# One merge-gate product of the convolution branch, computed among the indexer's scores

## The chip, the core and the metric

The kernel runs on one core of a Trainium2 chip. The metric is the device time of one execution in microseconds. A core has a matrix engine (PE, with its weight loads as PEld), a vector engine (DVE), an activation engine (ACT), a general engine (POOL) and an engine that issues transfers (SP). Each works through its own instruction list strictly in order, and an instruction whose input isn't there holds up all behind it on its engine.

## The reference, cut to what matters

One decoder block on 1024 tokens and 16 meta tokens (L = 1040), width 1024. Between two feed-forward halves stands a hybrid mixer:

```python
q, k, v, qi, ki, wi, u, gate_b, gate_c, g_att, g_conv = jnp.split(h @ w_in, offs, axis=-1)
# indexer: I[t,s] = sum_h wi[t,h] relu(qi[t,h] . ki[s]); keep the 256 best causal keys; GQA attention on them
s = jax.nn.relu(jnp.einsum('bthd,bsd->bths', qi, ki))
score = jnp.einsum('bths,bth->bts', s, wi)
y_att = att @ w_att_out
y_conv = (gate_b * short_conv(gate_c * u, conv_w)) @ w_conv_out
merged = jax.nn.sigmoid(g_att) * y_att + jax.nn.sigmoid(g_conv) * y_conv
return merged @ w_o
```

The product in question is an eighth of `g_conv = h @ w_in[:, O_GB:]`: 128 of its 1024 channels, for all 1024 real tokens.

## The kernel before

Activations lie as channels by tokens, every float32 operand split into a high and a low part, so that a product is three matmuls a step (`hi*xh`, `hi*xl`, `lo*xh`). A weight slab of 1024x128 is loaded by SP into a tile `raw` (L147), rounded by ACT into `hi` (L142), and its rest put into `lo` by DVE or POOL (L143). Times 1024 tokens that is 2 halves x 8 steps x 3 = 48 matmuls of 512 columns (L169 to L171, into a bank `ps`). The slabs of one pool (`slots`) go through two buffers each of `raw`, `hi` and `lo`; a third load waits until the first is used up.

The stages that the change touches, in their order:

1. Indexer queries (`queries`, O_QI): products, rotary on DVE, casts `rh` on ACT and rests `rl` on DVE, then stores of both to DRAM (`qis`, L747, issued by SP). Each store has 32 partitions x 4 heads x 512 tokens. Then the values (`values`): products, copies `v_t` on ACT, transposes (L724), casts into the same `rh`/`rl` buffers, stores `vd` (L733).
2. Indexer scores (`scores`), token tiles 7 to 1: PE computes a chunk into one of three banks `acc` (L760, L761), ACT takes the relu (L763), DVE weighs and adds it (L766, L768). A list BETWEEN says what product is issued after each tile's scores. In the kernel before it asks for the four attention query products (`"0011"`, stores `qs`) after the last tile, and for nothing before. The framework's scheduler then places each engine's instructions by its own estimate, so products that are written later also stand among the scores on PE.
3. Convolution: four slabs of channels k, each with products u, C and B. After the B product of a slab come, in a chain, a copy `tap` on ACT (L865), a multiplication on POOL (L866), a cast into `ah` on ACT (L142) and its rest `al` on POOL (L143). In the traces the tiles `self.yh` and `self.yl` of the convolution are named `ah` and `al`.
4. `conv_out`, m = 0 to 7: the gate product of 48 matmuls, then 24 matmuls with `w_conv_out` on `ah`/`al` (all four slabs k), sigmoid, multiplication on POOL (L888), store to `z` (L889).
5. Under stages 3 and 4, DVE searches each token's threshold (L793 to L815) and makes the masks (`keep`, L829 to L836). The search's first instruction waits for the last `qs` stores, whose SBUF it reuses.
6. Attention (`attend`): POOL loads a tile's queries (`q<-qs`, L915), PE makes the logits (L923, L924), DVE adds the mask (L926). Its first DVE instruction stands behind the last mask, and its first load behind the last L888.

```python
def gate_conv():
    m = next(early_gates)
    self.gate(rp, w, O_GB + 128 * m, self.z[m])
...
for i, what in zip(range(NT - 1, 0, -1), BETWEEN):
    self.scores(rp, i)
    for c in what.strip():
        between[c]()
```

`GB_EARLY` counts the letters g in BETWEEN. `gate` makes the product, copies it on ACT (L898) and stores it to DRAM (L899). `conv_out` computes its gate product only for m from GB_EARLY on; for smaller m SP loads it back from `z` (L880).

Of the kernel before, what the change touches and what calls it, by code (L numbers as in the profile page):

```python
# [26 lines left out]
DFF = 2816  # L27
FT = DFF // 128
TOPK = 256
BETWEEN = [" ", " ", " ", " ", " ", " ", "0011"]  # L30
GB_EARLY = "".join(BETWEEN).count("g")
LAG = 3
WIDE = L // 2
# [57 lines left out]
class Block:  # L91
# [919 lines left out]
    def mixer(self, early, wo1, stop=None):  # L1011
# [3 lines left out]
        with ExitStack() as mx:  # L1015
            mp = self.pool(mx, "mix")
            self.mask = [mp.tile([128, sum(c[1] for c in key_chunks(i))], BF16, name=f"mask{i}") for i in range(NT)]
            with ExitStack() as ab:
                sp = self.pool(ab, "scp")
                self.sc = [None] + [sp.tile([128, META + 128 * (i + 1)], F32, name=f"sc{i}") for i in range(1, NT)]  # L1020
                with ExitStack() as pa:
# [27 lines left out]
                    between["g"] = gate_conv  # L1049
                    for i, what in zip(range(NT - 1, 0, -1), BETWEEN):  # L1050
                        self.scores(rp, i)
# [382 lines left out]
```

## Time and profile before

| | us |
|---|---|
| median of 3 runs (lowest, highest) | 2288.71 (2286.47, 2289.03) |
| the profiled execution, its own time | 2292.01 |
| its span in the trace | 2290.1 |
| PE busy | 2188.5 (96%) |
| DVE busy | 1532.4 (67%) |
| ACT busy | 908.7 (40%) |
| POOL busy | 874.5 (38%) |

Busy times are sums of instructions' durations. Matmuls overlap their neighbours, so a busy PE can still be made shorter only where its list is. All places below are microseconds from the start of the span.

### The profile page before, as it was taken

Reading aid. Unit: us, or ns where it says so; the run is one execution under the profiler, and the core shown is the slowest. Engines: PE = TensorE matmul, PEld = TensorE weight load, DVE = VectorE, ACT = ScalarE, POOL = GpSimd, SP = SyncE. Lnnn points to the kernel's source line nnn. Section 1 sums busy time; section 2 is a strip of 40 time slices with the busy share of each in tenths; the row PEclk is TensorE's granted clock in tenths of the full one; section 3 lists DMA queues with packets and bytes.
Section 4 is the critical chain, followed back from the end, with each engine's and each line's share of the span. In section 5 each row is a group of like instructions: output and inputs, shape, how many; then the busy total and the mean of one; then the engine's idle time right before and its main releaser. Section 6 shows DMA issues by size and latency. Waiting matters only on the chain.

```text
span 2290.1 us, 31598 instructions
## 1 busy us (share of the span) xinstructions
PE 2188.5 (96%) x11708; PEld 1857.2 (81%) x11708; DVE 1532.4 (67%) x2716; ACT 908.7 (40%) x1497; POOL 874.5 (38%) x586
## 2 busy tenths in 40 slices
PE   6999999989999897999999999999999999989997
PEld 5999999987777786899887777777788888877775
DVE  6456565565786747699997887545555555566787
ACT  4434444442112426333224676432444434343213
POOL 2465555553222211155433100224346454563322
PEclk8999999999999898999999999999999999999999
DMA  3435435369575343341224211641153535369784
GB/s 116 135 111 163 142 128 177 105 233 332 190 265 164 113 132 92 116 97 45 74 69 102 60 43 54 211 168 65 61 188 104 191 110 183 120 210 337 235 266 146
DMA packets 299685, 335.02 MB, mean 146 GB/s; under 512 B 20432, under 2 KB 227948, under 8 KB 299148
## 3 DMA queue, kind: packets, MB, share of 16 engines
q1 hardware_dynamic: 230508, 243.33, 33.8%
q10 hardware_dynamic: 52976, 80.76, 9.8%
q0 software_dynamic: 16048, 8.93, 2.1%
q8 instruction: 92, 1.51, 0.3%
q14 instruction: 61, 0.50, 0.1%
HBM read 220.19 MB, written 112.76 MB: 145 GB/s over the span
## 4 chain that ended last, share of the span: by engine, by line
PE 53%; DVE 4%; DMA 3%; POOL 1%; issue 1%; ACT 1%; SPq 0%; DVEq 0%; ACTq 0%; POOLq 0%
PE a L269 14%; PE c L269 7%; PE ps L171 6%; PE ps L169 6%; PE ps L170 6%; PE b L269 3%; PE pt L958 2%; PE ps L1325 1%; PE ps L1326 1%; PE ps L1324 1%; PE po L949 1%; PE sc L923 1%; PE po L950 1%; DMA raw<-in_ffn_w_down_dram 1%; PE acc L760 1%
## 5 line engine op out<-in xcount | busy, mean ns | idle before, releaser
L143 DVE TENSOR_TENSOR lo<-raw,hi 128x1024 fp32r<-128x1024 f32 (+1 forms) x176 | 194.3, 1119 | 174.5 <-ACT hi L142 174.5
L142 ACT CAST hi<-raw 128x1024 fp32r<-128x1024 f32 (+1 forms) x219 | 188.2, 873 | 294.7 <-PE ps L170 81.4
L169 PE MATMUL ps<-xh,hi 128*128 128x512 f32 (+2 forms) x664 | 248.6, 374 | 0.3 <-DVE t L677 0.3
L171 PE MATMUL ps<-xh,lo 128*128 128x512 f32 (+2 forms) x664 | 248.5, 374 | 0.0
L170 PE MATMUL ps<-xl,hi 128*128 128x512 f32 (+2 forms) x664 | 248.3, 374 | 0.0
L793 DVE TENSOR_SCALAR_CACHE_REDUCE junk<-sc,cand 128x1040 uint8<-128x1040 f32 (+6 forms) x217 | 182.2, 893 | 0.0
L269 PE MATMUL c<-xh,hi 128*128 128x260 f32 (+1 forms) x704 | 176.1, 311 | 0.8 <-DVE T3l L192 0.8
L269 PE MATMUL c<-xh,lo 128*128 128x260 f32 (+1 forms) x704 | 176.1, 311 | 0.0
L269 PE MATMUL c<-xl,hi 128*128 128x260 f32 (+1 forms) x704 | 176.0, 311 | 0.0
L143 POOL TENSOR_TENSOR lo<-raw,hi 128x1024 fp32r<-128x1024 f32 (+1 forms) x43 | 87.3, 2031 | 207.0 <-ACT hi L142 206.9
L323 POOL TENSOR_TENSOR ws<-raw 128x512 f32<-128x512 f32 x40 | 53.0, 1326 | 263.2 <-DMA raw<-in_ffn_w_gate_dram 203.0
L269 PE MATMUL a<-xh,hl 128*128 128x512 f32 x416 | 145.6, 397 | 4.7 <-DVE y L595 3.0
L170 PEld LDWEIGHTS ps<-xl,hi 128*128 128x128 f32 x664 | 126.2, 190 | 17.0
L169 PEld LDWEIGHTS ps<-xh,hi 128*128 128x128 f32 x664 | 126.1, 190 | 16.8 <-DVE t L677 0.6
L171 PEld LDWEIGHTS ps<-xh,lo 128*128 128x128 f32 x664 | 125.7, 189 | 16.5
L595 DVE TENSOR_TENSOR y<-a,y 128x512 f32<-128x512 f32 x152 | 101.5, 686 | 41.3 <-PE a L269 40.9
L269 PE MATMUL a<-hi,hl 128*128 128x512 f32 x288 | 105.7, 411 | 20.0 <-DMA hl<-hd 8.1
L269 PEld LDWEIGHTS c<-xh,hi 128*128 128x128 f32 x704 | 114.4, 188 | 9.0 <-DVE T3l L192 1.0
L269 PEld LDWEIGHTS c<-xl,hi 128*128 128x128 f32 x704 | 114.5, 188 | 7.7
L269 PEld LDWEIGHTS c<-xh,lo 128*128 128x128 f32 x704 | 114.4, 188 | 7.8
L143 DVE TENSOR_TENSOR lo<-ws,hi 128x1024 fp32r<-128x1024 f32 x54 | 108.1, 2001 | 4.6 <-ACT hi L142 3.2
L234 POOL TENSOR_TENSOR y<-y,gb 128x1024 f32<-128x1024 f32 (+1 forms) x19 | 47.3, 2489 | 137.9 <-DVE y L233 71.2
(359 smaller groups left out, 5969.4 us busy)
## 6 DMA issues: line engine op xcount, KB each, us to landing
hl<-hd SPq DMA_DIRECT2D x280, 256.0 KB
hd<-hl ACTq DMA_DIRECT2D x154, 256.0 KB
hd<-hl ACTq DMA_DIRECT2D x77, 512.0 KB
raw<-in_ffn_w_gate_dram SPq DMA_DIRECT2D x44, 512.0 KB
raw<-in_ffn_w_up_dram SPq DMA_DIRECT2D x44, 512.0 KB
raw<-in_ffn_w_down_dram SPq DMA_DIRECT2D x44, 512.0 KB
raw<-in_w_in_dram SPq DMA_DIRECT2D x37, 512.0 KB
h<-y SPq DMA_DIRECT2D x15, 512.0 KB
```

Source lines behind the costliest of these rows:

```text
L142: self.nc.scalar.copy(hi, src)
L143: lo_eng.tensor_tensor(lo, src, hi.bitcast(F32), OP.subtract)
L169: mm(out, wh, xh, start=start, stop=False)
L170: mm(out, wh, xl, start=False, stop=False)
L171: mm(out, wl, xh, start=False, stop=stop)
L234: eng[1].tensor_tensor(y[:p], y[:p], b[:p], OP.add)
L269: self.nc.tensor.matmul(out, w, v, start=start and first, stop=last, skip_group_check=True)
L323: P.tensor_tensor(s[:, 512:], r2[:, :512], r2[:, 512:], OP.add)
L595: V.tensor_tensor(yv, ps, yv, OP.add)
L760: nc.tensor.matmul(ps[:, :n], q[:, h, :], self.ki1[:, o:o + n], start=True, stop=False)
L793: V.tensor_scalar(junk[:, :x.shape[1]], x, s, None, op0=OP.is_ge, op1=OP.add, accum_out=cnt[:, j:j + 1])
L958: nc.tensor.transpose(pt[:kw, m * r:m * r + m], ps_[r][q0:, 128 * kb:128 * kb + kw], self.ident[q0:, q0:])
```

## The change

The product for m = 0 is issued right after the scores of token tile 7, the first that is scored. `conv_out(0)` then loads it.

```diff
-BETWEEN = [" ", " ", " ", " ", " ", " ", "0011"]
+BETWEEN = ["g", " ", " ", " ", " ", " ", "0011"]
 GB_EARLY = "".join(BETWEEN).count("g")
```

What moves is seen in the engines' lists. SP's list before, at the end of the indexer queries (`rh0_8192` to `rl1_8195` belong to the last but one batch of stores, `rh0_8264` and so on to the last; `raw_9376` and `raw_9483` are the first convolution slabs):

```order
L147 DMA raw_9226<-in_w_in_dram 128x8x128
L747 DMA qis0_79<-rh0_8192 4x32x512
L747 DMA qis0_79<-rh1_8193 4x32x512
L747 DMA qis0_79<-rl0_8194 4x32x512
L747 DMA qis0_79<-rl1_8195 4x32x512
L747 DMA qis0_79<-rh0_8264 4x32x512
L747 DMA qis0_79<-rh1_8265 4x32x512
L747 DMA qis0_79<-rl0_8266 4x32x512
L747 DMA qis0_79<-rl1_8267 4x32x512
L147 DMA raw_9376<-in_w_in_dram 128x8x128
L147 DMA raw_9483<-in_w_in_dram 128x8x128
L733 DMA vd_85<-rh0_8366 128x4x64 x2
```

The same place after the change:

```order
L147 DMA raw_9288<-in_w_in_dram 128x8x128
L747 DMA qis0_79<-rh0_8192 4x32x512
L747 DMA qis0_79<-rh1_8193 4x32x512
L747 DMA qis0_79<-rl0_8194 4x32x512
L747 DMA qis0_79<-rl1_8195 4x32x512
L147 DMA raw_9128<-in_w_in_dram 128x8x128
L747 DMA qis0_79<-rh0_8264 4x32x512
L747 DMA qis0_79<-rh1_8265 4x32x512
L747 DMA qis0_79<-rl0_8266 4x32x512
L747 DMA qis0_79<-rl1_8267 4x32x512
L733 DMA vd_85<-rh0_8366 128x4x64 x2
```

A third load of the pool, `raw_9128` for the attention queries, now stands between the two batches, because the gate's slab has one of the two buffers; the two convolution slabs are gone from here and stand behind the gate's stores.

ACT's list before, at the same time (`hi_9056` and `hi_9058` are the attention queries' slabs):

```order
L142 CAST rh0_8192<-t0_8182 128x512
L142 CAST rh1_8193<-t2_8184 128x512
L142 CAST hi_9056<-raw_9060 128x8x64
L142 CAST hi_9056<-raw_9066 128x8x64
L142 CAST hi_9058<-raw_9060 128x8x64
L142 CAST hi_9058<-raw_9066 128x8x64
L142 CAST rh0_8264<-t0_8254 128x512
```

ACT's list after (`hi_8548` is the gate's slab):

```order
L142 CAST rh0_8192<-t0_8182 128x512
L142 CAST rh1_8193<-t2_8184 128x512
L142 CAST hi_8548<-raw_8546 128x1024
L142 CAST hi_9118<-raw_9122 128x8x64
L142 CAST hi_9118<-raw_9128 128x8x64
L142 CAST rh0_8264<-t0_8254 128x512
```

The cast that needs `raw_9128` now stands ahead of the last batch's `rh0_8264`, of the copies `v_t` and of all relus.

PE's list before, at the end of the last B product (`ps_10345`), where the gate product for m = 0 (`ps_10387`) follows:

```order
L169 MATMUL ps_10345<-xh_58,hi_10314 128x512
L170 MATMUL ps_10345<-xl_59,hi_10314 128x512
L171 MATMUL ps_10345<-xh_58,lo_10315 128x512
L169 MATMUL ps_10387<-xh_58,hi_10382 128x512
L170 MATMUL ps_10387<-xl_59,hi_10382 128x512
L171 MATMUL ps_10387<-xh_58,lo_10383 128x512
```

PE's list after, from the 16th matmul behind the last B product on (`ps_10454` and `ps_10471` are the two halves of `w_conv_out` for m = 0, `ps_10495` is the gate product for m = 1; the 15 ahead of these are three slabs k of the first half and two of the second):

```order
L169 MATMUL ps_10471<-ah_9464,hi_10450 128x512
L170 MATMUL ps_10471<-al_9465,hi_10450 128x512
L169 MATMUL ps_10454<-ah_9464,hi_10450 128x512
L171 MATMUL ps_10471<-ah_9464,lo_10451 128x512
L169 MATMUL ps_10471<-ah_9464,hi_10450 128x512
L169 MATMUL ps_10495<-xh_58,hi_10490 128x512
L170 MATMUL ps_10495<-xl_59,hi_10490 128x512
L170 MATMUL ps_10454<-al_9465,hi_10450 128x512
```

No product stands between the last B product and the matmuls on `ah`/`al` any more: the third row needs the last slab's `ah`, the last row its `al`. On POOL the split of the next gate slab, 1024 wide, now stands ahead of L866, where before a 512 wide one stood. Among the scores of tile 7 PE's list holds as many rows of L169 to L171 as before, now the gate's in place of the attention queries'; the gate's other 33 matmuls stand between tiles 7 and 6. From the gate product for m = 1 on the lists agree again.

## Rows read from the trace of the kernel before

**Rows 1.** Stretches: length, busy PE, PEld, DVE, ACT, POOL (instructions), PE clock, DMA share, GB/s

```profile
849.00:863.00 14.00, 10.11 (x64) 9.19 (x62) 6.99 (x12) 3.74 (x8) 0.00 (x0) 1.00 0.26 94
878.50:957.00 78.50, 78.50 (x387) 68.20 (x387) 67.70 (x127) 46.58 (x102) 13.96 (x13) 0.97 0.33 80
968.00:1178.70 210.70, 210.70 (x1072) 185.55 (x1070) 209.38 (x713) 61.33 (x88) 107.67 (x61) 1.00 0.30 78
```

**Rows 2.** Waits of PE from 860 to 985: total us, times, longest

```profile
PE acc L760 <- ACT relu L763: 12.0, 3, 6.0
```

**Rows 3.** Timeline of PE: a gate product's first matmul, the next product's, attention's first

```profile
1205.92 0.40 PE L169 MATMUL ps<-xh,hi 128*128 128x512 f32 x1
...
1217.12 0.39 PE L169 MATMUL ps<-ah,hi 128*128 128x512 f32 x1
...
1233.44 0.39 PE L923 MATMUL sc<-k,q 128*128 128x256 f32 x1 [3.01 <-DMA q<-qs]
```

**Rows 4.** Timeline of SP's transfers around the last indexer queries

```profile
831.61 2.36 SPq L147 DMA_DIRECT2D raw<-in_w_in_dram  x1
846.40 2.19 SPq L747 DMA_DIRECT2D qis<-rl  x2
852.01 2.77 SPq L747 DMA_DIRECT2D qis<-rh  x2
860.03 9.93 SPq L147 DMA_DIRECT2D raw<-in_w_in_dram  x2
870.05 2.78 SPq L733 DMA_DIRECT2D vd<-rh  x1
```

**Rows 5.** Timeline of ACT there

```profile
844.02 0.62 ACT L142 CAST hi<-raw 128x512 fp32r<-128x512 f32 x1 [10.54 <-DMA raw<-in_w_in_dram]
...
845.59 2.18 ACT L142 CAST hi<-raw 128x512 fp32r<-128x512 f32 x4
851.36 1.23 ACT L142 CAST rh<-t 128x512 fp32r<-128x512 f32 x2 [3.60 <-issue]
...
864.24 0.59 ACT L142 CAST rh<-pt 128x512 fp32r<-128x512 f32 x1 [6.27 <-DMA qis<-rh]
...
877.08 0.26 ACT L142 CAST rh<-pt 16x128 fp32r<-16x128 f32 x1 [3.67 <-DMA vd<-rh]
```

**Rows 6.** Timeline of DVE: in the scores, at the search's start, the last mask, attention

```profile
870.36 0.69 DVE L143 TENSOR_TENSOR rl<-pt,rh 128x512 fp32r<-128x512 f32 x1 [11.35 <-DMA qis<-rl]
...
967.95 1.24 DVE L793 TENSOR_SCALAR_CACHE_REDUCE junk<-sc 128x1040 uint8<-128x1040 f32 x1 [9.15 <-DMA qs<-rh]
...
1223.79 3.47 DVE L836 SCALAR_TENSOR_TENSOR mask<-lt,eq 128x1040 bf16<-128x1040 bf16 x1
1233.98 0.42 DVE L926 CUSTOM_DVE_ANT_0 p<-sc,mask 128x256 f32<-128x256 f32 x1 [6.72 <-PE sc L924]
```

**Rows 7.** Timeline of ACT and POOL behind the last B product, and PE's first matmul on `ah`

```profile
1091.29 0.59 ACT L865 COPY tap<-ps 128x512 f32<-128x512 f32 x1 [2.52 <-POOL acc L860]
...
1096.17 1.05 ACT L142 CAST ah<-acc 128x1024 fp32r<-128x1024 f32 x1 [3.29 <-POOL acc L866]
...
1092.47 1.30 POOL L143 TENSOR_TENSOR lo<-raw,hi 128x512 fp32r<-128x512 f32 x1 [1.22 <-ACT hi L142]
1093.73 2.40 POOL L866 TENSOR_TENSOR acc<-acc,tap 128x1024 f32<-128x1024 f32 x1
1097.30 2.40 POOL L143 TENSOR_TENSOR al<-acc,ah 128x1024 fp32r<-128x1024 f32 x1 [1.16 <-ACT ah L142]
...
1100.58 0.39 PE L169 MATMUL ps<-ah,hi 128*128 128x512 f32 x1
```

**Rows 8.** Chain that ended last, where attention begins: start, us, what

```profile
1228.35 5.04 DMA q<-qs
```

**Rows 9.** A wait of PE in the last feed-forward half, and the stretch behind it

```profile
2046.12 0.47 PE L269 MATMUL a<-hi,hl 128*128 128x512 f32 x1 [4.04 <-DMA hl<-hd]
...
2047.50:2050.50 3.00, 3.00 (x9) 2.32 (x8) 3.00 (x4) 0.62 (x1) 3.00 (x3) 0.50 1.01 289
```

## The prediction

> **What bounds the kernel now.** I read the busy times by stretch first, since the page's shares mix stages. From 878.5 to 957 PE is busy for all of the 78.50 us at a clock of 0.97, and from 968 to the end of the search both PE and DVE are full (210.70 and 209.38 of 210.70) [rows 1]. So a matmul moved out of the second stretch is worth something there only if the first has room for it, and DVE's search may not start later for nothing. Then I looked for room: PE's waits in the scores come to 12.0 us in three pieces, all on relus [rows 2]. The timelines of ACT and DVE tell why the relus are late: casts into the buffers `rh` and `rl` stand ahead of them and wait for the stores of the indexer queries and values to land, until 864.24 and 877.08 on ACT and 870.36 on DVE [rows 5, 6]. The transfers in that time move 94 GB/s at a share of 0.26 [rows 1]. Last I read the place where the search, the convolution and attention meet. The search starts at 967.95 behind the last query stores, the last mask ends at 1223.79 + 3.47 = 1227.26, and DVE then sits idle for 6.72 us until attention's first logits [rows 6]. PE waits 3.01 us there for the query load [rows 3], which POOL issues at 1228.35, behind its last multiplication, and which takes 5.04 us [rows 8]. So PE, through POOL, sets when attention begins, and the search has 6.7 us to spare.
>
> **The product itself.** A gate product is 48 matmuls: 1217.12 - 1205.92 = 11.20 us [rows 3]. They leave `conv_out(0)` and come into the scores. PE's list shows 15 of them among tile 7's scores, at the places where the attention queries' matmuls stood, and 33 in a block behind. So the waits of [rows 2] are not filled any better: what stood there and what stands there are equally many. PE is full from 878.5 on, so queries, convolution and everything behind start 11.20 us later, and `conv_out(0)` gives the 11.20 us back. Sum on PE: 0. The ACT copies, the stores to `z`, the loads back and the two sigmoids (0.59 us each by the like-sized copies [rows 7]) lie beside full PE stretches on engines that are busy for 46.58 of 78.50 and 61.33 of 210.70 us [rows 1]. I take them at nothing; if they were uncovered they'd cost about 2 us.
>
> **The search** starts with the last query stores, so 11.20 us later, and it isn't shortened. Its end moves to 1227.26 + 11.2 = 1238.5, which is 4.5 us past the 1233.98 at which attention's first DVE instruction starts now. So even if nothing else goes wrong, the change costs 4.5 us here, unless PE is later still.
>
> **The third slab load.** The gate's slab takes one of two `raw` buffers, so the second half of the queries' slab can load only when the gate's slab is split. By the rows: ACT is free for the gate's cast at 845.59 [rows 5], which takes 1.05 us like `ah` [rows 7]; POOL's rest takes 2.40 [rows 7]; so SP can issue the load at 849.1, just behind the stores that it has issued by 846.40 + 2.19 = 848.6 [rows 4]. The nearest load is the one of the same size at 831.61, also right behind such a batch; ACT got it at 844.02, after 12.4 us [rows 4, 5]. So ACT's next cast waits until 861.5, and the last `rh`, which it makes at 851.36 now, comes at 862.1: 10.8 us late. Queued behind it on ACT are the copies `v_t`, which PE's transposes wait for, and all relus.
>
> How much of the 10.8 us arrives at the scores? Now the stores issued at 852.01 stand behind the earlier batch, and DVE gets its buffer at 870.36 [rows 4, 6]. After, they find the queue empty at about 863: three of four stores are 0.79 MB, 8 us at the 94 GB/s of [rows 1], and with some 3 us for a transfer's ends that is 874 to 876, 4 to 6 us late. The third wait, ACT's until 877.08, is for a `vd` store that SP could only issue at 870.05, behind 9.93 us of issuing two convolution slabs [rows 4]. Those two loads are moved behind the gate's stores, so that store goes earlier, and ACT no longer stands the 3.67 us. So 5 - 3.67, about 1.3, and up to 2.5 if the store, now queued behind the late batch, is still awaited. I take **2.0 us**. Bounds: -3.7, if the load is there in time and only the third wait goes, and +6, if nothing is given back.
>
> A page says otherwise: the Trainium skill, "DMA: Bandwidth & Descriptors", section "Anatomy of one DMA", fits a transfer issued from GpSimd as 2.0 us plus its bytes at 436 GB/s; as an estimate by that page the 512 KB would land 3.2 us after issue, at 852.3, and this step would be a gain. No row here shows a slab load behind query stores that quick; the row's 12.4 us decides, and the page's case is the second rival below.
>
> **The lost cover at conv_out(0).** The last slab's `ah` and `al` are made while PE computes the gate product for m = 0. That cover is gone. The last B product ends at 1100.58 - 11.20 = 1089.38 [rows 3, 7]. In PE's new list 17 matmuls follow that need nothing new, 17 x 11.20 / 48 = 3.97 us, to 1093.35. Then `ah` is needed. Now it is there at 1096.17 + 1.05 = 1097.22 [rows 7]. On POOL a 1024-wide split now stands ahead of L866 in place of the 512-wide one of 1.30 us [rows 7], and the 512-wide one stands where the wide one stood, a few instructions ahead; the two trade places in one chain, so I leave the times as they are. PE waits 3.9 us, runs five matmuls (1.17 us) to 1098.4, and waits for `al` until 1097.30 + 2.40 = 1099.70: 1.3 more. Sum **5.2 us**. The bounds: 6.3 if the wide split costs its extra 1.1 us in full; 3.4 if POOL does L866 right behind the first `tap` (1091.88 + 2.40 + 1.05 + 2.40 = 1097.7 for `al`, against 1094.3 by then issued). This is in no list hidden by other matmuls.
>
> After such a wait the clock falls. The wait of 4.04 us before 2046.12 is followed by 3.00 us at a granted clock of 0.50, that is 1.2 GHz [rows 9], in which PE does half its work: **1.5 us** lost. Bounds 0 and 2. The Trainium skill, "TensorE: Matmul & The Clock Gate", Part 1, says that the half clock is the default and that activity releases it; the trace agrees. Without that the sum would be 7.2 instead of 8.7.
>
> **The sum.** 0 + 2.0 + 5.2 + 1.5 = 8.7 us on PE's way to attention. The search's way: 11.2 + 2.0 puts its end to 1240.5, while PE's way brings attention's first DVE instruction to 1233.98 + 8.7 = 1242.7. So PE's way still decides, by 2.2 us, and the two don't add. Behind that the lists are the same and nothing absorbs it. The profiled execution's own 2292.01 (span 2290.1) becomes 2300.7; it lies 3.3 above the median of the runs, so the median 2288.71 becomes **2297.4**.
>
> **Rivals.**
> - *The search decides.* If PE's waits at `conv_out(0)` are hidden or short, DVE's late end sets attention: 1240.5 - 1233.98 = 6.5 us, 2295.2. For it: DVE is full throughout. Against: 2.2 us are missing.
> - *The slab load is in time.* Then only the third wait goes: -3.7 + 6.7 = 3.0, 2291.7 (the search alone: 1238.5 - 3.7 - 1233.98 = 0.8). For it: most DMA engines are idle at a share of 0.26. Against: the 12.4 us of the load at 831.61 at the same share.
> - *The late load costs in full.* 6 + 6.7 = 12.7, 2301.4, and a few more if the clock stays low longer. For it: the relus of 20 chunks stand behind that cast. Against: the third wait is relieved.
> - *The gate fills the waits of the scores* (not slower). If matmuls of the gate ran in the 12.0 us in which PE waits for relus, up to 11.2 us would come for nothing, and 6.7 - 11.2 = -4.5, 2284.2, would remain; it decides from 6.7 us filled on. For it: the waits are there. Against: PE takes its list in order, and the matmuls stand behind the same waiting scores as before.
>
> **Chances.** My forecast 0.55 (its own range 2294 to 2302), the search 0.14, the load in time 0.13, the late load in full 0.11, the filled waits 0.07. About 0.2%, 4.6 us, is what a measurement here can tell from no change: 2284.1 to 2293.3. The load in time lies mostly within it, the filled waits mostly just below, the others above: faster 0.05, same 0.16, slower 0.79. The range reaches from the load in time nearly to its lower end, with the clock's and the wait's low bounds, to the late load in full with the upper ones (6 + 6.3 + 2 = 14.3, with the runs' spread): 2289 to 2305.
>
> **What would show it.** In the changed profile: a wait of ACT for `raw` until about 861 ahead of the last `rh`, and no wait for `vd` later; PE waits of some 4 and 1 us ahead of the first matmuls on the last slab's `ah` and `al`, with a clock of 0.50 behind; the search starting some 13 us later; DVE's idle time ahead of attention shrunk from 6.72 to about 2 us; attention's first matmul near 1242. I am wrong if the query slab lands by 853, if the products on `ah` run without a wait, or if PE finishes the scores with its waits filled.

## The result, and the profile after

The changed kernel takes 2301.25 us in the median of 5 runs (2294.43 to 2309.23), against 2288.71 of the kernel before in the same session: the ratio is 1.0053, with a 95% interval of 1.0036 to 1.0070, that is 12.1 us slower (8.2 to 16.0). Run once more it came to 1.0038 (1.0025 to 1.0051), 8.7 us (5.7 to 11.7). The forecast was 8.7. The profiled execution has a span of 2299.3 us.

First, PE's waits from 800 to 1250 in the changed kernel: who waited for whom, total us, times, longest.

```profile
PE pt L724 <- ACT v_t L718: 8.0, 1, 8.0
PE acc L760 <- ACT relu L763: 4.8, 2, 2.7
PE ps L169 <- ACT ah L142: 3.7, 1, 3.7
PE sc L923 <- issue: 2.6, 1, 2.6
PE ps L171 <- POOL lo L143: 1.6, 1, 1.6
```

The scores' waits of 12.0 us [rows 2] are 12.8 us now, under other names: 8.0 of them for `v_t`. Two waits are new, 3.7 for the last slab's `ah`, which was forecast, and 1.6 for a split on POOL, which was not.

The third slab load, on SP's timeline (start us, us of issuing, what):

```profile
841.74 1.12 SPq L747 DMA_DIRECT2D qis<-rh  x2
845.93 2.86 SPq L147 DMA_DIRECT2D raw<-in_w_in_dram  x1
859.91 1.12 SPq L747 DMA_DIRECT2D qis<-rh  x2
862.98 5.12 SPq L733 DMA_DIRECT2D vd<-rh  x2
```

and on ACT's (start us, us, what, in brackets the idle time ahead and what ended it):

```profile
842.13 1.56 ACT L142 CAST hi<-raw 128x1024 fp32r<-128x1024 f32 x2
858.75 0.62 ACT L142 CAST hi<-raw 128x512 fp32r<-128x512 f32 x1 [15.05 <-DMA raw<-in_w_in_dram]
859.28 1.13 ACT L142 CAST rh<-t 128x512 fp32r<-128x512 f32 x2
874.91 0.25 ACT L142 CAST rh<-pt 16x128 fp32r<-16x128 f32 x1 [0.53 <-DMA vd<-rh]
...
1004.09 1.28 ACT L881 ACT_TABLE_LOAD   x1 [7.76 <-DMA sig<-z]
1006.92 1.03 ACT L142 CAST hi<-raw 128x1024 fp32r<-128x1024 f32 x1
...
1106.65 1.04 ACT L142 CAST ah<-acc 128x1024 fp32r<-128x1024 f32 x1 [4.33 <-POOL acc L866]
```

The load is issued behind the batch of stores that begins at 841.74, as forecast. Issued at 845.93, it lets ACT go on at 858.75, after 12.8 us (12.4 were taken), and ACT stood 15.05 us for it. The wait for a `vd` store, 3.67 us before [rows 5], is down to 0.53, since the `vd` stores now follow the last query stores on SP at once, at 862.98. DVE gets the buffer for which it waited until 870.36 before [rows 6] at

```profile
871.33 0.69 DVE L143 TENSOR_TENSOR rl<-pt,rh 128x512 fp32r<-128x512 f32 x1 [7.69 <-DMA qis<-rl]
```

The row at 1004.09 is the one that the forecast had left out: the sigmoid on the gate that is loaded back waits 7.76 us, and the cast of a weight slab stands behind it. SP took long to issue the two loads:

```profile
990.00 8.48 SPq L880 DMA_DIRECT2D sig<-z  x2
```

On POOL:

```profile
1008.03 2.36 POOL L143 TENSOR_TENSOR lo<-raw,hi 128x1024 fp32r<-128x1024 f32 x1 [9.23 <-ACT hi L142]
...
1233.53 1.28 POOL L888 TENSOR_TENSOR sig<-yc,sig 128x512 f32<-128x512 f32 x1
1234.76 1.57 POOL L915 DMA_DIRECT2D q<-qs  x2
```

and on PE, where `conv_out(0)` and attention's first matmul are shown as well:

```profile
1010.45 0.42 PE L171 MATMUL ps<-xh,lo 128*128 128x342 f32 x1 [1.63 <-POOL lo L143]
...
1103.66 0.39 PE L170 MATMUL ps<-al,hi 128*128 128x512 f32 x1
1107.75 0.80 PE L169 MATMUL ps<-ah,hi 128*128 128x512 f32 x1 [3.70 <-ACT ah L142]
...
1110.22 0.79 PE L170 MATMUL ps<-al,hi 128*128 128x512 f32 x1
...
1113.64 0.40 PE L169 MATMUL ps<-xh,hi 128*128 128x512 f32 x1
...
1239.22 0.36 PE L923 MATMUL sc<-k,q 128*128 128x256 f32 x1 [2.61 <-issue]
```

From 1107.75 to 1113.64 PE issues 13 matmuls in 5.89 us, where at the full clock they take 13 x 0.233 = 3.03 [rows 3]. The busy times by stretch give the granted clock there (length, then busy PE, PEld, DVE, ACT, POOL, PE clock, DMA share, GB/s):

```profile
1103.90:1107.70 3.80, 0.14 (x1) 0.00 (x0) 3.80 (x13) 1.04 (x1) 2.72 (x2) 0.86 0.54 138
1107.70:1113.60 5.90, 5.85 (x13) 4.20 (x14) 5.90 (x19) 1.69 (x3) 3.85 (x3) 0.51 0.00 0
```

So behind the wait the clock is 0.51, the lower of its two levels, 1.2 GHz, as in [rows 9]. PE is busy for 5.85 of these 5.90 us, so what they take beyond 3.03 is nearly all the clock's, and hardly any of it a wait for `al`. Last DVE, at the search's start and at attention's:

```profile
978.20 1.24 DVE L793 TENSOR_SCALAR_CACHE_REDUCE junk<-sc 128x1040 uint8<-128x1040 f32 x1 [10.72 <-DMA qs<-rh]
...
1235.94 1.24 DVE L836 SCALAR_TENSOR_TENSOR mask<-lt,eq 128x1040 bf16<-128x1040 bf16 x1
1239.74 0.42 DVE L926 CUSTOM_DVE_ANT_0 p<-sc,mask 128x256 f32<-128x256 f32 x1 [2.55 <-PE sc L924]
```

The search starts at 978.20, still behind a `qs` store. DVE's spare time ahead of attention fell from 6.72 [rows 6] to 2.55 us. PE still decides, by that much, and through POOL as before: it issues the query load at 1234.76, behind its last multiplication.

Traces of one kernel differ by some us ahead of the scores, so places are counted from here on from the first store of indexer queries (`qis`) on SP. The table has, in us, the convolution's first copy (L846 on ACT), the search's first instruction and attention's first on DVE, and the time against the kernel before, measured in the same session.

| kernel | first store at | convolution | search | attention | ratio, 95% |
|---|---|---|---|---|---|
| before | 813.4 | 145.3 | 154.5 | 420.6 | 1 |
| before, again | 810.0 | 142.4 | 151.8 | 417.5 | 1 |
| changed | 809.9 | 157.4 | 168.3 | 429.8 | 1.0053 (1.0036 to 1.0070) |
| changed, again | 808.3 | 156.2 | 167.1 | 428.7 | 1.0038 (1.0025 to 1.0051) |
| 1: m = 4 | 810.9 | 156.3 | 167.2 | 423.5 | 1.0024 (1.0015 to 1.0034) |
| 2: other pool | 812.9 | 157.1 | 163.0 | 426.2 | 1.0039 (1.0024 to 1.0053) |
| 3: both | 809.6 | 159.8 | 165.7 | 426.2 | 1.0019 (1.0008 to 1.0031) |
| 4: cover only | 813.4 | 142.5 | 152.0 | 425.7 | 1.0039 (1.0026 to 1.0052) |
| 5: ahead of scores | 811.9 | 152.3 | 161.8 | 419.1 | 1.0011 (1.0002 to 1.0021) |
| 6: behind queries | 814.8 | 157.8 | 157.2 | 420.6 | 1.0002 (0.9991 to 1.0012) |
| 7: two products | 813.0 | 167.7 | 173.8 | 429.4 | 1.0057 (1.0036 to 1.0078) |
| 8: own buffers, 3 | 815.0 | 127.2 | 127.3 | 402.1 | 0.9940 (0.9921 to 0.9959) |
| 9: own buffers, 2, and the change | 810.0 | 157.9 | 158.5 | 428.6 | 1.0038 (1.0025 to 1.0051) |
| 10: own buffers, 2 | 812.8 | 141.3 | 141.4 | 416.3 | 1.0004 (0.9991 to 1.0016) |

### The profile page after: what moved, and what is told of

Same layout as the page of the kernel before. It is cut to its first block, busy times and chain, and to the rows that moved or that the text cites. A ratio compares the mean times of both kernels' runs of the same rounds, so it can differ in the third digit from the quotient of the medians.

```text
span 2299.3 us, 31602 instructions
## 1 busy us (share of the span) xinstructions
PE 2192.6 (95%) x11708; PEld 1860.6 (81%) x11708; DVE 1540.1 (67%) x2716; ACT 909.7 (40%) x1499; POOL 871.8 (38%) x586
## 4 chain that ended last, share of the span: by engine, by line
PE 68%; DVE 17%; issue 5%; DMA 5%; POOL 3%; ACT 2%; SPq 0%; ACTq 0%; DVEq 0%; POOLq 0%
PE a L269 29%; PE c L269 17%; DVE junk L793 8%; PE b L269 4%; PE ps L170 2%; PE ps L171 2%; PE ps L169 2%; PE pt L958 2%; PE ps L1325 1%; PE ps L1326 1%; PE ps L1324 1%; PE po L949 1%; PE b L606 1%; PE sc L923 1%; DMA hl<-hd 1%
## 5 line engine op out<-in xcount | busy, mean ns | idle before, releaser
L171 PE MATMUL ps<-xh,lo 128*128 128x512 f32 (+2 forms) x664 | 248.0, 374 | 1.6 <-POOL lo L143 1.6
L169 PE MATMUL ps<-xh,hi 128*128 128x512 f32 (+2 forms) x664 | 248.3, 374 | 0.4 <-DVE t L677 0.4
L171 PEld LDWEIGHTS ps<-xh,lo 128*128 128x128 f32 x664 | 125.6, 189 | 18.4 <-POOL lo L143 1.9
L169 PEld LDWEIGHTS ps<-xh,hi 128*128 128x128 f32 x664 | 125.9, 190 | 17.0 <-DVE t L677 0.6
```

The costliest lines, as they stand in the source:

```text
L169: mm(out, wh, xh, start=start, stop=False)
L171: mm(out, wl, xh, start=False, stop=stop)
```

## The experiments

Kernels 1, 2, 3, 6, 7 and 9 are edits of the changed kernel, 4, 5, 8 and 10 of the kernel before. All do the same products in full.

**Both kernels once more.** For the changed one:

> The changed kernel once more, for a second trace and more times. If the terms that its first trace shows are all there is (2.0 us of late scores, 1.6 us of a wait for a split behind the sigmoids on the loaded gate, 6.6 us of lost cover with the slow clock), attention begins 10.3 us later than before, counted from the first query product, and the time is 10 to 11 us above that of the kernel before. Rival: the first trace's stretch behind attention, 5.1 us longer than before, is also the change's; then the time is 13 to 15 us above, and the stretch is long again.

and for the one before:

> The kernel before once more, for a second trace of it. It tells how far the stretches from start to queries and from attention to the end differ between two traces of one kernel: if by 4 to 5 us, the like differences between the first traces of before and after are not the change's; if by under 1 us, they are.

The changed kernel's 8.7 us are nearest to the first case. The two traces of before differ by 3.4 us ahead of the first query store and by 3.1 us from there to attention, and the second has 9.9 us of PE waits in the scores where the first has 12.0:

```profile
PE acc L760 <- ACT relu L763: 9.9, 3, 4.9
```

Against their mean, 419.0, attention begins 10.8 and 9.7 us late in the two traces of the changed kernel; 10.3 were expected. From attention's first DVE instruction to the end it takes 1056.1 and 1057.2 us before, 1059.6 and 1062.5 after (the first is 3.4 us longer than the first of before, not 5.1); over all 14 traces it ranges from 1054.7 to 1062.5, so whether a few us there are the change's can't be told from these traces.

**1. The cover kept: m = 4 is the early product.**

```diff
-early_gates = iter(range(GB_EARLY))
+early_gates = iter(range(4, 4 + GB_EARLY))
-gs = None if m < GB_EARLY else self.slab(w, O_GB + 128 * m, nc.gpsimd)
+gs = None if 4 <= m < 4 + GB_EARLY else self.slab(w, O_GB + 128 * m, nc.gpsimd)
```

> The early product is that for m = 4 instead of m = 0, so conv_out(0) keeps its gate product as cover, and the loaded gate is wanted only later. Forecast's theory, two ways to attention: the wait for the last slab's casts and the wait behind the sigmoids go (8.2 us on PE), but the search still starts 14 to 15 us later and ends about 14 us later, so attention begins 7 to 8 us later than before, only 2 to 3 us earlier than in the changed kernel. Rival, PE alone counts: attention begins 2 us later than before, 8 us earlier than in the changed kernel.

5.5 us above before (3.4 to 7.8), between the 8.7 and 12.1 us of the changed kernel and the 2 us of the rival: both waits behind the scores are gone, and DVE has no spare time left. The row of PE's waits and DVE's timeline:

```profile
PE sc L923 <- DVE mx L926: 4.5, 1, 4.5
```

```profile
1233.24 1.24 DVE L836 SCALAR_TENSOR_TENSOR mask<-lt,eq 128x1040 bf16<-128x1040 bf16 x1
1234.40 0.42 DVE L926 CUSTOM_DVE_ANT_0 p<-sc,mask 128x256 f32<-128x256 f32 x1
```

Attention's first logits follow the last mask without a gap, and PE waits for DVE: the search decides. That attention is only 4.5 us late and not 7 to 8 goes with a shorter search: from its first instruction to the end of the last mask it takes 256.4 us here and 259.3 in both traces of before (see the last section).

**2. The slab in time: the gate's slab from the other pool.**

```diff
-gs = self.slab(w, col, nc.gpsimd)
+gs = self.slab(w, col, nc.gpsimd, slots=slots)   # slots=self.ext for the early product
```

> The gate's slab comes from the other pool of buffers, so the second half of the queries' slab loads in time, and the scores begin as before. Forecast's theory: ACT's wait for raw ahead of the last rh goes and its 3.7 us wait for a vd store comes back; the convolution begins 11.2 us later than before instead of 13.2, and the time is 2 us under that of the changed kernel, 8 to 9 us above before. Rival, the late load in full: 6 us under the changed kernel. Rival, the late load costs nothing: no difference.

ACT's wait for `raw` is gone and the wait for the `vd` store is back:

```profile
876.54 0.26 ACT L142 CAST rh<-pt 16x128 fp32r<-16x128 f32 x1 [3.87 <-DMA vd<-rh]
```

but the convolution begins at 157.1, where it began at 157.4 and 156.2 with the late slab, and PE's waits in the scores come to 13.3 us:

```profile
PE acc L760 <- ACT relu L763: 10.6, 3, 4.6
PE pt L724 <- DVE rl L143: 2.7, 1, 2.7
```

So the step's mechanism is there, but on PE's way it costs nothing against a slab in time: "the late load costs nothing" holds for the convolution. It doesn't hold for the search, which begins at 163.0 here and at 168.3 and 167.1 with the late slab. The time, 8.9 us above before (5.5 to 12.1), can't be told from that of the changed kernel. Attention begins 2.5 to 3.6 us earlier all the same. The wait behind the loaded gate, 1.6 us, isn't among PE's waits here, and the stretch at the low clock behind `ah` was shorter (1108.54 to about 1112.0, against 1107.75 to about 1113.4).

**3. Both.**

> Both edits of the two kernels above. Forecast's theory: PE has lost nothing (0), the search starts and ends 11.2 us later, has 6.7 us to spare, and attention begins 4.5 us later than before: 4 to 5 us above the kernel before, with DVE full up to attention's first logits and PE waiting there. Rival, PE alone counts: no difference from before. Rival, something in the moved product's stores or copies costs by itself: 8 us or more above.

4.4 us above before (1.8 to 7.1), as the theory has it. The one trace fits less well: against the mean of before the search begins 12.5 us late, not 11.2, and attention 7.2. From 1100 to 1250 PE waits for nothing but

```profile
PE sc L923 <- DVE mx L926: 3.2, 1, 3.2
PE sc L923 <- issue: 2.0, 1, 2.0
```

**4. The lost cover alone.** In `conv_out(0)` of the kernel before the gate product is written behind the products with `w_conv_out`; the multiplications and stores for m = 0 follow it, and nothing is moved out of the stage.

```diff
+if m:
+    gate()
 ws = self.slab(self.a["w_conv_out"][0], 128 * m, nc.gpsimd, kt=4)
...
+if not m:
+    gate()
```

> The kernel before, with one order turned round: conv_out(0) issues its products with w_conv_out first and its gate product behind them, so no product is moved out of the stage and nothing is loaded back, and only the cover of the last slab's casts is gone. Forecast's theory: PE waits some 4 us for ah and about 1 us for al, then runs at the low clock for a few matmuls, 6.6 us in all; the search is as before and has 6.7 us and more to spare, so attention begins 6.6 us later and the time is 6 to 7 us above before. Rival, the two waits in the changed kernel come from its moved slabs and not from the lost cover: no difference from before.

8.9 us above before (6.0 to 11.9). PE's timeline shows the two waits, 17 matmuls behind the last B product and 5 further on; DVE's shows how long the search had been done (new lines shift L926 to L935):

```profile
1094.47 0.50 PE L169 MATMUL ps<-ah,hi 128*128 128x512 f32 x1 [3.73 <-ACT ah L142]
...
1096.93 0.80 PE L170 MATMUL ps<-al,hi 128*128 128x512 f32 x1 [0.72 <-POOL al L143]
```

```profile
1239.08 0.42 DVE L935 CUSTOM_DVE_ANT_0 p<-sc,mask 128x256 f32<-128x256 f32 x1 [15.51 <-PE sc L933]
```

The search is 15.51 us ahead here, so this is PE's path alone, and by its time it costs as much as the whole change; in its trace attention begins 6.7 us late, as expected. The two costs lie side by side: 4.4 us on DVE's way (kernel 3), 8.9 on PE's. Their sum, 13.3, lies above the second interval of the changed kernel and within the first, so the times alone don't show that only the larger counts. DVE does: in both traces of the changed kernel it still waits for PE ahead of attention, 2.55 and 2.19 us.

**5. The product ahead of the scores**, with the edits of 3, no `g` in BETWEEN and GB_EARLY set to 1:

```diff
+gate_conv()
 for i, what in zip(range(NT - 1, 0, -1), BETWEEN):
```

> The early product (m = 4, slab from the other pool) is written ahead of the scores of tile 7 instead of behind them, so on PE all its 48 matmuls stand ahead of the first score. If PE's 12 us of waits among the first scores come from relus that are held up until about 877 whatever PE does, the 11.2 us of the product lie in them: search and queries start within 1 us of before, PE reaches attention 11 us earlier, the search then decides, and attention begins 6 to 7 us earlier than before: time 5 to 7 us below before. Rival, the scores pay for the product as they do behind tile 7: search 11.2 us later, time 4 to 5 us above before, as with the two edits together.

2.5 us above before (0.5 to 4.8). Search and convolution begin 8.6 and 8.5 us later than in the mean of before, between the two expectations, so of the product's 11.2 us less than 3 were filled; attention, at 419.1, isn't late in this trace. ACT's timeline:

```profile
878.60 0.26 ACT L142 CAST rh<-pt 16x128 fp32r<-16x128 f32 x1 [13.24 <-DMA vd<-rh]
878.76 0.57 ACT L898 COPY gate<-ps 128x512 f32<-128x512 f32 x1
...
880.24 1.12 ACT L763 ACTIVATE relu<-acc 128x346 f32<-128x346 f32 x3
```

Now all relus stand behind the third cast, which waits for a `vd` store, and PE waits 9.74 us for the first of them until 880.74. SP's timeline tells why that store is late:

```profile
861.23 9.02 SPq L147 DMA_DIRECT2D raw<-in_w_in_dram  x2
870.34 4.82 SPq L733 DMA_DIRECT2D vd<-rh  x2
```

Two convolution slabs are issued ahead of it, in 9.02 us. The third cast comes 66.7 us behind the first query store, where it came after 63.7 and 61.7 in the traces of before, and no relu runs ahead of it any more. So PE had filled the early waits with the product, but stands for the relus until the cast all the same.

**6. The product behind the last queries**, m = 4:

```diff
-BETWEEN = ["g", " ", " ", " ", " ", " ", "0011"]
+BETWEEN = [" ", " ", " ", " ", " ", " ", "0011g"]
```

> The early product (m = 4) is written behind the last attention queries instead of behind tile 7. PE has the same work as with m = 4 behind tile 7, but the search starts as before. Forecast's theory, the delayed search is what is left of the cost: search and attention begin within 1 us of before, and the time is within 2 us of before, 4 to 5 us below the kernel with m = 4 behind tile 7. Rival, the moved product's own copies, stores and loads cost: still 4 to 5 us above before.

0.5 us above before (-2.1 to 2.7), 5.0 below kernel 1. The search doesn't begin within 1 us of the mean of before, as expected, but 4.0 us later, and attention 1.6; DVE still waits 2.23 us for PE ahead of attention. So the same product on the same engines, with stores, copies and loads, costs nothing that can be measured if it delays the search by less than it has to spare and leaves `conv_out(0)` its cover.

**7. Two products**, m = 4 and 5, on top of 3:

```diff
-BETWEEN = ["g", " ", " ", " ", " ", " ", "0011"]
+BETWEEN = ["g", "g", " ", " ", " ", " ", "0011"]
```

> Two early products (m = 4 behind tile 7, m = 5 behind tile 6, slabs from the other pool), conv_out(0) with its cover. Theory, the search's late start less the 6.7 us that it had to spare: search 22.4 us later than before, attention and the end 15 to 16 us later, 11 us more than with one product. Rival, each early product costs the same by its own copies, stores and loads: twice what one cost, 9 us above before. Rival, PE alone counts: no difference.

13.1 us above before (8.2 to 17.9), an interval that holds the theory's 15 to 16 and the first rival's 9 alike. That PE alone counts is out: it waits for DVE for

```profile
PE sc L923 <- DVE mx L926: 9.5, 1, 9.5
```

The search starts 8.1 us later than with one product, not 11.2; in the one trace of kernel 3 PE waited 15.1 us in the transposes and scores, here 13.2. Attention begins 10.4 us later than in the mean of before. What each further product costs stays loosely measured.

**8. Buffers of their own for the values' casts**, in the kernel before:

```diff
-vh = pool.tile([128, 512], F32R, name="rh0", bufs=2)
-vl = pool.tile([128, 512], F32R, name="rl0", bufs=2)
+vh = pool.tile([128, 512], F32R, name="vh", bufs=3)
+vl = pool.tile([128, 512], F32R, name="vl", bufs=3)
```

> The kernel before, no early product, but the values' casts have three buffers of their own instead of those of the query stores, so neither ACT nor DVE waits for a store ahead of the relus. If those waits are what held PE in the first scores, its 10 to 12 us of waits go and the clock stays high there: queries, search, convolution and attention all begin 10 to 13 us earlier, and the time is 10 to 13 us below before. Rival, the relus are held by something else (the scores' query loads, DVE's own work): the wait is there under another name, and the time is within 3 us of before.

13.7 us below before (9.4 to 18.1): the fastest of all. PE has no wait in the scores, and from 848 to 880 it is full at the full clock:

```profile
848.00:880.00 32.00, 31.60 (x176) 28.63 (x176) 29.23 (x56) 24.22 (x53) 1.33 (x3) 1.00 0.63 154
```

In the kernel before the same stretch has waits and a lower clock:

```profile
848.00:880.00 32.00, 19.52 (x92) 17.06 (x92) 13.98 (x27) 9.63 (x23) 0.00 (x0) 0.73 0.49 135
```

So more goes than the waits. The convolution begins 16.6 us earlier than in the mean of before, of which 9.9 to 12.0 are waits; the rest goes with the clock, which was 0.73 there; the two weren't varied apart. The search also begins with the convolution, at 127.3, instead of 9 us behind it, probably because the buffers lie elsewhere in memory; that wins nothing by itself, since DVE waits for PE ahead of attention here too (in kernel 10, which has the same early search, the time is that of before).

**9 and 10. Two such buffers**, with and without the change:

> The changed kernel (m = 0, behind tile 7) with two buffers for the values' casts of their own. In the changed kernel the late query slab was nearly hidden (2 us), because what it held up would have waited for the stores anyway. Theory: without these waits it is bare. ACT still waits for raw until some 47 us behind the first query store, PE waits 8 us for v_t, and the search starts 11 us later for the product and some 8 us later for the slab than in the kernel before with buffers of its own: 13 to 17 us above that kernel, 2 to 4 us above the kernel before. Rival, the late slab costs 2 us by itself: the same 9 us above the kernel with buffers of its own as the change costs otherwise, so some 2 us below before.

> The kernel before with two buffers of their own for the values' casts instead of three: the partner of the run above, without the early product. The two waits for query stores go, but the third cast still needs the first values store, which stands on SP behind the loads of two convolution slabs. Theory: ACT still waits there, until about 62 us behind the first query store, PE waits 3 to 6 us once, and the time is 6 to 10 us below before; the early product then costs 14 to 18 us against this kernel, because the late slab is bare. Rival, the third wait is covered: 12 to 14 us below, as with three buffers.

Kernel 10 gains nothing (0.9 us above, -2.1 to 3.7), against both expectations. ACT's timeline, and PE's waits:

```profile
873.78 0.26 ACT L142 CAST vh<-pt 16x128 fp32r<-16x128 f32 x1 [13.00 <-DMA vd<-vh]
```

```profile
PE acc L760 <- ACT relu L763: 13.0, 1, 13.0
```

The waits for the query stores are gone and the third has grown from 3.67 to 13.00 us. It ends 61.0 us behind the first query store, where it ended after 63.7 and 61.7 before: the three end in one place, set by the `vd` store. Kernel 9 is 8.7 us above before (5.7 to 11.7), more than both of its expectations, and so about 8 us slower than kernel 10, not 14 to 18. With ACT's third cast at

```profile
874.86 0.25 ACT L142 CAST vh<-pt 16x128 fp32r<-16x128 f32 x1 [6.39 <-DMA vd<-vh]
```

the late slab lies under this wait again, in part: the convolution begins 16.6 us later than in kernel 10, 5.4 more than the product, and attention 12.3. My theory for 9 and 10, that the first two waits were the slab's cover, fell; some cover is left with the third alone. What the bare slab costs, with three buffers, wasn't tried and stays open.

## Why the prediction held, step by step

**The product, 0 on PE:** right. The convolution begins 13.0 us later than in the mean of the two traces of before (156.8 against 143.8), and `conv_out(0)` gives 11.2 back.

**The third slab load, 2.0:** 13.0 - 11.2 = 1.8 us remain at the convolution's start, so the size fits, and each place on the way too. Counted from the first query store, the load is issued at 36.0 us (35.7 forecast) and ACT goes on at 48.8 (48.1); DVE's buffer comes 4.4 us late (4 to 6), and the `vd` wait is down to 0.53. But the prediction weighed the three waits as if each had its own worth ("so 5 - 3.67"). Kernel 10 shows that the last one, for the `vd` store, decides, and kernel 2 agrees: with the slab in time 2.1 us remain (157.1 - 143.8 - 11.2). What is left of it lies within the 3 us by which the two traces of before differ here, so that 2.0 was met is in part luck. The 3 us that the prediction took for a transfer's ends stand in none of its rows. Nor did it count the lower clock among the scores, 0.73 in kernel 8's stretch; it is there before and after, so little of it enters the difference. The estimate by the Trainium skill, "DMA: Bandwidth & Descriptors", section "Anatomy of one DMA", 3.2 us for a transfer of this size issued from GpSimd, is not met by this one: 12.8 us, on SP's queue behind stores.

**The loads back at nothing:** this is the term that was mis-sized. I took ACT's sigmoids as work beside full PE stretches and did not ask what is queued behind them. They stand in ACT's list ahead of a weight slab's cast; the load waited on SP behind the loads of `k` and `vs` and took 8.48 us to issue, and PE lost 1.6 us (1.9 in the second trace). The prediction named 2 us as the price without cover, but of the copies and sigmoids themselves, not of a cast behind them; that the size is near is luck.

**The lost cover, 5.2, and the clock, 1.5:** 3.70 us for `ah` (3.9 forecast), then 5.89 - 3.03 = 2.86 for `al` and the clock together (1.3 and 1.5), nearly all of it the clock's: at the low clock PE comes to `al` later and hardly waits for it. Sum 6.6, in the second trace 5.8; forecast 6.7. Kernel 4 shows it alone, with 7.5 us. (The forecast's low bound, 3.4, comes to 3.2 by its own terms: five matmuls behind 1093.35 end at 1094.5, not 1094.3.)

**The search as the second way, 2.2 us behind PE's:** right, 2.55 and 2.19 us. Take PE's waits away (kernels 1 and 3) and it decides; delay the search by less than it has to spare (kernel 6) and nothing is lost that can be measured.

**The sum:** 1.8 + 1.6 + 6.6 = 10.0 us at attention's start, where the traces show 10.8 and 9.7; forecast 8.7. The first time, 2301.25, is nearer to the 2301.4 of "the late load costs in full" than to the forecast, so the number alone doesn't tell these two apart. The convolution's start does: 1.8 us remain there, and that rival has 6. That the second measurement is 8.7 to the digit is chance. "The load is in time" is kernel 2, which wins none of the 5.7 us of that rival. Of the others, "the search decides" is what kernels 1 and 3 are, and "the gate fills the waits" fails even with the product ahead of the scores (kernel 5).

## What to carry to other kernels

When several waits follow one another on one engine, ask which of them ends last and what sets that end: removing the earlier ones only lengthens it (kernel 10), removing all three gains (kernel 8). Removing the last alone wasn't tried. A product that is moved on a full engine costs whatever it delays beside it and whatever it had covered where it stood; in this kernel these two prices lie on different ways to the same meeting point, and the larger counts. A load that replaces work belongs into the list of the engine that consumes it: look at what is queued behind its first use.

## What was not expected of the hardware

The last mask (L836, 128x1040) took 3.47 us before [rows 6] and 1.24 after. Its chain from L829 on took 12.4 us before (1214.88 to 1227.26), 11.9 after and 7.1 in kernel 1 (1227.34 to 1234.48). Before, POOL was at splits and multiplications beside it until it issued the query load at 1228.35 [rows 8]; in kernel 1 it had done its last at 1225.2. Over the 14 traces the chain takes 7.1 us in the five in which POOL splits and multiplies nothing beside it, or only under its last instruction (kernels 1, 3, 4, 5 and 7), and 10.4 to 12.7 in the nine others. The Trainium skill, "SBUF — State Buffer", section "Who interferes with whom", has a rule that fits: a DVE instruction with two inputs in SBUF and a POOL instruction that reads SBUF exclude each other. This rule doesn't cover L830, which has one such input and a number for each partition and still took 0.76 us or, beside POOL in five traces, 1.6 to 3.0. So up to 5 us of this chain hang on what POOL does just then. That this is why attention came earlier than expected in kernel 1 is likely, not shown: its whole search was 2.9 us shorter, and that of kernel 3, with the same short chain, was 1.3 us longer than before.

Issuing a slab load took SP 0.37 to 0.38 us in quiet stretches (in kernel 2, at 981.12 and 992.28) and 7.4 to 9.9 us for two behind a batch of stores (7.38 in kernels 2 and 10, 9.93 before [rows 4]); an engine's list that looks idle by its transfers' bytes can be late by the issuing alone.
